# A two-layer hybrid trunk on one core: weight slots of the token-wise blocks shifted by 448 bytes, three raw buffers for four, and transposes moved out of the 256-column matmul streams

## Chip, cores, metric

One core of one Trainium2 chip. The time is the device time of one execution in microseconds, and it is compared as the median of several executions. Inputs and weights lie in the chip's memory as float32, and the output goes back there.

## What is computed

Two layers; in each, the 256 tokens of 1024 channels pass a gated feed-forward block, a mixer and another feed-forward block, each followed by a LayerNorm of `alpha*x + block(x)`. Cut to what matters:

```python
def swiglu(x, w1, w2):
    g, u = jnp.split(x @ w1, 2, axis=-1)          # w1: 1024 x 5632, w2: 2816 x 1024
    return (jax.nn.silu(g) * u) @ w2

def hybrid_mixer(x, w_in, b_merge, sc_w, rc_w, rc_b, rg_w, rg_b, a_param, w_out_conv, w_out_rnn, w_o):
    b_gate, c_gate, v, x_r, y_r, g_logits = jnp.split(x @ w_in, SPLITS, axis=-1)
    y_a = (b_gate * causal_depthwise_conv(c_gate * v, sc_w, 3)) @ w_out_conv
    xc = causal_depthwise_conv(x_r, rc_w, 4) + rc_b
    gates = jax.nn.sigmoid(per_head(xc, rg_w) + rg_b)         # 4 heads of 256
    h = rg_lru(xc, gates[0], gates[1], a_param)               # a scan over the tokens
    y_b = (h * jax.nn.gelu(y_r)) @ w_out_rnn
    g_a, g_b = jnp.split(jax.nn.sigmoid(g_logits + b_merge), 2, axis=-1)
    return (g_a * y_a + g_b * y_b) @ w_o

for l in range(2):
    x = layer_norm(ALPHA * x + 0.5 * swiglu(x, ffn_w1[l, 0], ffn_w2[l, 0]), ...)
    x = layer_norm(ALPHA * x + hybrid_mixer(x, ...), ...)
    x = layer_norm(ALPHA * x + 0.5 * swiglu(x, ffn_w1[l, 1], ffn_w2[l, 1]), ...)
```

## The kernel before

**Precision by three products.** Every float32 matrix is split into two parts in a matmul format (`F32R`): `hi`, the rounded value, and `lo`, what rounding left. A product is the sum hi·hi + hi·lo + lo·hi, so each matmul of the mathematics is three on TensorE.

**Units of weights.** All weights stream through the core once, in units of 1 MB (128 partitions x 2048 floats). `load_unit` takes a buffer `raw` (pool `praw`, `NRAW` of them) and one each of `hi` and `lo` (six of each, `NBUF`), and issues the load on SyncE's queue. `high` makes `hi` on ScalarE (L202), `low` makes `lo` on VectorE (L207); when `low` is done the raw buffer is free for a later load. Units are issued in the program's order, up to six (`LOOK`) ahead of those that TensorE has used up.

**Two forms of matmul.** In the channel-wise form (`mm_cols`, L219) a 128x128 piece of the weights is the stationary operand and 256 tokens of x (or of an intermediate) are the moving one: 256 columns, output transposed, channels on partitions. One unit is 48 such matmuls. In the token-wise form, 128 tokens are stationary and 512 columns of the weights move. The second matmul of each block (`form_b`, tile `acc`) has this form, and so have the first weight units of every block (`filler`, tile `fill`): token-wise they can begin on the first half of the tokens while the LayerNorm of the second half still runs.

**What follows the fill.** Its output has tokens on partitions and has to be transposed by TensorE (fp32 matmuls against an identity) for what comes next. In a feed-forward block `fill_transposes` (tile `hT`, L439) does this for the h of the first 256 channels, one step into the `gu` stream (gate and up projections); the first feed-forward block has two such fill blocks (`NFILL`), the others one. In the mixer the fill is 512 columns of the x_r projection; `x_transposes` (L500) turns them back in two groups of four, one behind `c0` and one behind `v0` of the order `MIX`.

**The order.** `MIX` lists the mixer's steps: `c v b` and `wc` are the gated convolution and its output projection, `x` and `rg` the recurrent branch, `sqrt` and `lru` its elementwise part and scan (VectorE, with some ScalarE), `y` the gelu branch, `ga gb` the merging gates, `wr` the recurrent output projection. `form_b` closes each block: its first units run over all outputs, the last three (`LAG`) output by output, so that LayerNorm can begin early. The steps are handed to a scheduler, which may move independent instructions past each other on an engine, matmuls too.

**Intermediates** lie in slots of 2 KB per partition (pool `act`, `NSLOT` of them), or, for eight of the wide ones, in the constant tiles `yh` and `yl`, from where `wc`, `rg` and `wr` take them as moving operand and `form_b` as stationary one (with a shift of 16 floats, L457).

**Addresses.** In the built program of before, taken modulo 512 bytes, xh, xl, yh and yl rows begin at 128, and all hi and lo buffers at 192; yh and yl rows with the shift of 16 floats, and all slots, at 192. So in `acc` the moving and the stationary operand begin at the same place modulo 512 (192 and 192); in `fill` they do not (weights 192, x 128), nor in the 256-column streams (x 128, weights 192).

**The start.** `opening` warms TensorE up and takes the first two units in halves; the loads go on one queue in this order: x and units 0 and 1, six small loads of bias and gate vectors (`load_vectors`), then units 2, 3, and so on.

Of the kernel before, what the change touches and what calls it, by code (L numbers as in the profile page):

```python
# [13 lines left out]

P = 128
NBUF = 6
NRAW = 4
NSLOT = 14
LAG = 3
LOOK = 6  # L20
WARM = 8
# [2 lines left out]
MIX = [  # L24
    (t.rstrip("0123"), int(t[-1]) if t[-1].isdigit() else 0)
    for t in (
        "c0 x0 v0 x1 x2 x3 rg0 c1 rg1 b0 v1 rg2 b1 rg3 sqrt c2 v2 b2 c3 v3 b3 lru0 gb0 lru1 "
        "wc0 wc1 wc2 lru2 wc3 ga0 ga1 lru3 ga2 ga3 y0 y1 y2 y3 gb1 gb2 gb3 wr0 wr1 wr2 wr3"
    ).split()
]  # L30

# [1 line left out]
class Unit:  # L33


    def __init__(self, srcs, shape):
        self.srcs, self.shape = srcs, shape


@with_exitstack  # L40
def trunk_kernel(
# [137 lines left out]
    def unit_half(parts, h):  # L179

        n = 512 // len(parts)
        srcs = []
        for i, (w, c0) in enumerate(parts):
            s = w[h * 512 : (h + 1) * 512, c0 : c0 + n].rearrange("(k p) c -> p k c", p=P)
            srcs.append((i * n, s))
        return unit(srcs, (4, 512))

    def load_unit(u, parts=1):
        u.raw = praw.tile([P, 2048], F32, tag="raw", name="raw")
        u.hi = phi.tile([P, 2048], F32R, tag="hi", name="hi")  # L190
        u.lo = plo.tile([P, 2048], F32R, tag="lo", name="lo")
        view = lambda t: t.rearrange("p (a b) -> p a b", b=u.shape[-1])
        u.h, u.l = view(u.hi), view(u.lo)
        n = u.shape[0] // parts
        for i in range(parts):
            ks = slice(i * n, (i + 1) * n)
            for c0, src in u.srcs:
                u.load = nc.sync.dma_start(out=view(u.raw)[:, ks, c0 : c0 + src.shape[-1]], in_=src[:, ks])
# [9 lines left out]
        gate[1] = max(gate[1] - 1, 0)  # L208

    def emit_unit(u):  # L210
        load_unit(u)
        high(u)
        low(u)

# [84 lines left out]
            elif t == 0:  # L299
                transpose_x(t, hh)  # L300

    def form_b(us, stat, c, l, n, last):

        Q = len(us)
        cuts = [[(0, 512), (512, 512)] for _ in range(NT)]
        if last:
            cuts[NT - 1] = [(0, 512), (512, 256), (768, 256)]
        acc = {}

        def pe(q, t, i):  # L310
            c0, n_ = cuts[t][i]
            if q == 0:
                acc[t, i] = bank("acc")[:, :n_]
            for kk in range(2):
                sh, sl = stat(q, kk, t)
                wh, wl = us[q].h[:, kk, c0 : c0 + n_], us[q].l[:, kk, c0 : c0 + n_]
                mm(acc[t, i], sh, wh, q == 0 and kk == 0, False)
                mm(acc[t, i], sl, wh, False, False)
                mm(acc[t, i], sh, wl, False, q == Q - 1 and kk == 1)

        for q in range(Q - LAG):
            step(lambda q=q: [pe(q, t, i) for t in range(NT) for i in range(len(cuts[t]))],
                 (lambda: load_gb(l, n, us[0])) if q == 0 else None, 1, [us[q]])
        for t in range(NT):
            for i in range(len(cuts[t])):
                for q in range(Q - LAG, Q):
# [77 lines left out]
    def ffn(l, i, n, last):  # L404
        w1, w2 = ffn_w1[l, i], ffn_w2[l, i]
        hs = {}
        opens = (l, i) == (0, 0)
        nfill = NFILL if opens else 1
        fill = [unit_half([(w1, 256 * b), (w1, DFF + 256 * b)], h) for b in range(nfill) for h in range(2)]
        ga, up = {}, {}  # L410
        for j in range(nfill, NPF):
            ga[j] = unit_a(w1, 256 * j)
            up[j] = unit_a(w1, DFF + 256 * j)
        us = [unit_b(w2, q) for q in range(NPF)]

        def swish(g, u, shape, name):

            v = slot(name)
            o = v.rearrange("p a b -> p (a b)")[:, : shape]
            nc.scalar.activation(o, g, AF.Tanh, scale=0.5)  # L420
            nc.vector.scalar_tensor_tensor(o, o, 1.0, g, op0=ALU.add, op1=ALU.mult)
            nc.vector.tensor_mul(o, o, u)  # L422
            return v

        tok = {}

        def post_fill(t, b, ps):
            tok[t, b] = swish(ps[:, 0:256], ps[:, 256:512], 256, "hf")

        filler(fill, post_fill, not opens)  # L430

        def fill_transposes(b):
            ps = bank("hT")
            h, lo = slot("h0h", F32R), slot("h0l", F32R)
            for t in range(NT):
                v = tok[t, b].rearrange("p a b -> p (a b)")
                for c in range(2):
                    with tc.issue_after(last_mm[0]):
                        nc.tensor.transpose(  # L439
                            ps[:, c * S + t * P : c * S + (t + 1) * P], v[:, c * P : (c + 1) * P], ident  # L440
                        )
# [23 lines left out]
        form_b(us, lambda q, kk, t: [v[:, kk, t * P : (t + 1) * P] for v in hs[q]], 0.25, l, n, last)  # L465


    def mixer(l, n):
        w = w_in[l]
        fill = [unit_half([(w, 3 * D)], h) for h in range(2)]  # L470
        cols = {"c": (w, D), "v": (w, 2 * D), "b": (w, 0), "x": (w, 3 * D), "y": (w, 4 * D), "ga": (w, 5 * D), "gb": (w, 6 * D),
                "wc": (w_out_conv[l], 0), "wr": (w_out_rnn[l], 0)}
        U = {}
        for key, j in MIX:
            if key in cols and (key, j) not in (("x", 0), ("x", 1)):
# [10 lines left out]
        B = {}  # L486

        def post_fill(t, b, ps):
            T["xt", t, b] = slot("xt").rearrange("p a b -> p (a b)")
            nc.scalar.copy(T["xt", t, b], ps)  # L490

        filler(fill, post_fill, True)

        def x_transposes(j):
            B["x", j] = bank("x")
            for c in range(2):
                for t in range(NT):
                    o = (j % 2) * 256 + c * P
                    with tc.issue_after(last_mm[0]):
                        nc.tensor.transpose(  # L500
                            B["x", j][:, c * S + t * P : c * S + (t + 1) * P], T["xt", t, j // 2][:, o : o + P], ident
                        )

        def proj(key, j):
# [79 lines left out]
        def lru(hd):  # L584


            s, y, e = T["s", hd], T["y", hd], T["xc", hd]
            d, q, a = slot("d"), slot("q"), slot("a")
            nc.scalar.activation(q, y, AF.Square)
            nc.vector.scalar_tensor_tensor(d, s, 1.0, y, op0=ALU.add, op1=ALU.mult)  # L590
            nc.vector.reciprocal(d, d)
            nc.vector.tensor_add(q, q, s)
            nc.vector.tensor_mul(q, q, d)
            nc.scalar.activation(a, q, AF.Square)
            nc.vector.scalar_tensor_tensor(a, s, 1.0, a, op0=ALU.add, op1=ALU.mult)
            nc.scalar.activation(a, a, AF.Copy, scale=-0.5, bias=1.0)
            nc.vector.tensor_mul(q, q, e)
            nc.vector.tensor_copy(q[:, :, 0:1], e[:, :, 0:1])
            for c in range(2):
                nc.vector.tensor_tensor_scan(d[:, c, :], a[:, c, :], q[:, c, :], 0.0, op0=ALU.mult, op1=ALU.add)  # L600
            T["h", hd] = d

        def post_y(j):

# [48 lines left out]
        for key, j in MIX:  # L653
# [2 lines left out]
                step(None, sqrt_all)  # L656
            elif key == "lru":
                step(None, lambda j=j: lru(j))
            elif key == "x" and j < 2:
                step(lambda j=j: x_transposes(j), after)  # L660
# [68 lines left out]
```

## Time and profile before

| | us |
|---|---|
| median of 3 executions | 1221.95 |
| the three | 1215.23, 1221.95, 1225.82 |
| the profiled execution: its time | 1216.33 |
| its span, first to last instruction | 1214.6 |
| TensorE matmul busy / weight loads busy | 1203.7 / 1138.0 |
| VectorE / ScalarE / GpSimd busy | 820.1 / 590.8 / 14.9 |
| granted TensorE clock, mean | 0.998 |
| DMA | 236.31 MB, mean 195 GB/s |

TensorE is busy 99% of the span, yet a busy engine is not one at its best pace: matmuls overlap, so how long one lasts says less than how far apart the starts are. A row of the timeline or of the chain of waits that merges N matmuls of a kind gives this: its length divided by N. Times in the chain are where the pieces of the chain that ended last begin and how long they are.

### The profile page before, as it was taken

How to read it: one execution, taken by the hardware profiler on the slowest of the kernel's cores; microseconds unless marked ns; L12 is line 12 of the kernel's file. 1: busy time of each engine (PE TensorE's matmuls, PEld its weight loads, DVE VectorE, ACT ScalarE, POOL GpSimd, SP SyncE). 2: the span in 40 equal slices, each digit the busy share in tenths (PEclk: the TensorE clock that was granted, in tenths of full speed). 3: DMA queues.
4: the chain of work that ended last, by engine and by line, in shares of the span. 5: the costliest groups of instructions: out<-in, count | busy, mean ns of one | idle time of the engine just before them, and what ended most of it. 6: DMA issues, size and time to landing. Idle time of an engine off the chain costs nothing.

```text
span 1214.6 us, 20489 instructions
## 1 busy us (share of the span) xinstructions
PE 1203.7 (99%) x8995; PEld 1138.0 (94%) x8995; DVE 820.1 (68%) x786; ACT 590.8 (49%) x566; POOL 14.9 (1%) x20
## 2 busy tenths in 40 slices
PE   8999999999999999999999999999999999999997
PEld 6999988999999899998899998899999998999986
DVE  5865547957997785564585554578789966856533
ACT  5644334775575354443254443266756744544420
POOL 0000000000000000000000000000000000000000
PEclk9999999999999999999999999999999999999999
DMA  8966563756566566655566655555665753856510
GB/s 282 328 217 217 176 205 100 248 186 229 176 209 213 169 194 218 215 207 177 169 194 217 216 207 177 170 187 174 223 206 184 243 175 103 278 188 229 201 43 35
DMA packets 186133, 236.31 MB, mean 195 GB/s; under 512 B 4076, under 2 KB 168124, under 8 KB 186044
## 3 DMA queue, kind: packets, MB, share of 16 engines
q1 hardware_dynamic: 186044, 235.00, 58.7%
q8 instruction: 70, 1.15, 0.4%
q14 instruction: 19, 0.16, 0.0%
HBM read 233.94 MB, written 1.05 MB: 193 GB/s over the span
## 4 chain that ended last, share of the span: by engine, by line
PE 97%; DMA 1%; DVE 0%; ACT 0%; SPq 0%; issue 0%; DVEq 0%; ACTq 0%
PE gu L216 35%; PE acc L216 23%; PE fill L216 5%; PE c L216 4%; PE v L216 4%; PE wr L216 4%; PE gb L216 4%; PE y L216 4%; PE ga L216 4%; PE wc L216 4%; PE b L216 4%; PE x L216 2%; PE rg L216 2%; DMA raw<-in_ffn_w_dram 1%; PE xT L262 1%; DVE lo L207 0%
## 5 line engine op out<-in xcount | busy, mean ns | idle before, releaser
L207 DVE TENSOR_TENSOR lo<-raw,hi 128x2048 fp32r<-128x2048 f32 (+1 forms) x218 | 493.5, 2269 | 231.9 <-ACT hi L202 230.7
L202 ACT CAST hi<-raw 128x2048 fp32r<-128x2048 f32 (+1 forms) x217 | 411.4, 1901 | 453.0 <-issue 170.0
L216 PE MATMUL gu<-xh,hi 128*128 128x256 f32 x1248 | 168.6, 277 | 0.0
L216 PE MATMUL gu<-xh,lo 128*128 128x256 f32 x1248 | 168.0, 277 | 0.0
L216 PE MATMUL gu<-xl,hi 128*128 128x256 f32 x1248 | 168.0, 277 | 0.0
L216 PEld LDWEIGHTS gu<-xh,hi 128*128 128x128 f32 x1248 | 154.5, 188 | 0.3
L216 PEld LDWEIGHTS gu<-xl,hi 128*128 128x128 f32 x1248 | 154.1, 188 | 0.0
L216 PEld LDWEIGHTS gu<-xh,lo 128*128 128x128 f32 x1248 | 154.1, 188 | 0.0
L216 PE MATMUL acc<-hi,hl 128*128 128x512 f32 (+1 forms) x196 | 73.8, 376 | 0.0
L216 PE MATMUL acc<-hi,hh 128*128 128x512 f32 (+1 forms) x196 | 73.7, 376 | 0.0
L216 PE MATMUL acc<-lo,hh 128*128 128x512 f32 (+1 forms) x196 | 73.7, 376 | 0.0
L422 DVE TENSOR_TENSOR hv<-hv,gu 128x512 f32<-128x512 f32 x39 | 26.8, 688 | 53.4 <-PE gu L216 53.2
L216 PE MATMUL acc<-hi,yh 128*128 128x512 f32 (+1 forms) x136 | 51.5, 379 | 0.0
L216 PE MATMUL acc<-hi,yl 128*128 128x512 f32 (+1 forms) x136 | 51.3, 377 | 0.0
L216 PE MATMUL acc<-lo,yh 128*128 128x512 f32 (+1 forms) x136 | 51.3, 377 | 0.0
L266 ACT CAST xh<-xT 128x512 fp32r<-128x512 f32 x24 | 13.4, 588 | 75.2 <-PE xT L262 74.8
L288 DVE SCALAR_TENSOR_TENSOR xtok<-acc,xtok 128x512 f32<-128x512 f32 (+1 forms) x25 | 16.7, 668 | 46.6 <-PE acc L216 46.3
L216 PEld LDWEIGHTS acc<-lo,hh 128*128 128x128 f32 x196 | 36.9, 188 | 6.8
L216 PEld LDWEIGHTS acc<-hi,hh 128*128 128x128 f32 x196 | 36.9, 188 | 6.7
L216 PEld LDWEIGHTS acc<-hi,hl 128*128 128x128 f32 x196 | 36.9, 188 | 6.7
L216 PE MATMUL fill<-hi,xh 128*128 128x512 f32 x112 | 30.6, 395 | 2.1 <-ACT hi L202 1.1
L216 PE MATMUL fill<-lo,xh 128*128 128x512 f32 x112 | 30.8, 397 | 0.2 <-DVE lo L207 0.2
(181 smaller groups left out, 1826.6 us busy)
## 6 DMA issues: line engine op xcount, KB each, us to landing
raw<-in_ffn_w_dram SPq DMA_DIRECT2D x122, 1024.0 KB, 5.2
raw<-in_w_in_dram SPq DMA_DIRECT2D x56, 1024.0 KB, 5.2
raw<-in_ffn_w_dram SPq DMA_DIRECT2D x16, 512.0 KB, 4.9
raw<-in_w_out_conv_dram SPq DMA_DIRECT2D x8, 1024.0 KB, 5.5
raw<-in_w_out_rnn_dram SPq DMA_DIRECT2D x8, 1024.0 KB, 5.5
raw<-in_w_o_dram SPq DMA_DIRECT2D x8, 1024.0 KB, 5.0
raw<-in_rg_w_dram SPq DMA_DIRECT2D x4, 1024.0 KB, 5.4
gB<-in_ln_g_dram SPq DMA_DIRECT2D x6, 512.0 KB, 6.3
```

Of the source, the lines that this page charges most:

```text
L202: (copy or nc.scalar.copy)(u.hi[:, part], u.raw[:, part])
L207: nc.vector.tensor_sub(u.lo[:, part], u.raw[:, part], f(u.hi[:, part]))
L216: last_mm[0] = nc.tensor.matmul(ps, lhs, rhs, start=first, stop=last).ins
L262: nc.tensor.transpose(ps[:, i * P : (i + 1) * P], xtok[:, t, c * P : (c + 1) * P], ident)
L266: nc.scalar.copy(dh, v)
L288: nc.vector.scalar_tensor_tensor(zc, ps, c, zc, op0=ALU.mult, op1=ALU.add)
L422: nc.vector.tensor_mul(o, o, u)
```

## The change

1. `NRAW` 4 to 3, `NSLOT` 14 to 15. Each hi and lo buffer grows by `PAD` = 128 floats, and units made by `unit_half` (those of the fills) begin `OFF` = 112 floats = 448 bytes into theirs. In the built program hi and lo buffers still begin at 192 modulo 512; the fill's weights then begin at 128, like the rows of x that they are multiplied with. No other operand moves modulo 512.
2. `fill_transposes` goes from the `gu` stream into `form_b`, behind its second unit; `form_b` takes the units in the order qs, so that the fill's h come eighth (first block: seventh and eighth).
3. In the mixer the fill is the first 512 columns of the g_b gate instead of x_r. `x0` and `x1` become ordinary units; `gb0` and `gb1` are transposed just before `wr0`, in one group of eight. `gb0` no longer stands behind `lru0`, and `sqrt` stands later.
4. `lru` works in place: its outputs overwrite s, its temporaries y and d. The operations are the same in number and size; Square now follows the first VectorE operation in place of going beside it.
5. Unit 2 is loaded ahead of the small vectors.

```diff
-NRAW = 4
-NSLOT = 14
+NRAW = 3
+NSLOT = 15
+PAD = 128
+OFF = 112
...
-        "c0 x0 v0 x1 x2 x3 rg0 c1 rg1 b0 v1 rg2 b1 rg3 sqrt c2 v2 b2 c3 v3 b3 lru0 gb0 lru1 "
-        "wc0 wc1 wc2 lru2 wc3 ga0 ga1 lru3 ga2 ga3 y0 y1 y2 y3 gb1 gb2 gb3 wr0 wr1 wr2 wr3"
+        "c0 x0 x1 v0 x2 x3 rg0 c1 rg1 b0 v1 rg2 b1 rg3 c2 v2 b2 c3 v3 b3 sqrt lru0 lru1 "
+        "wc0 wc1 wc2 lru2 wc3 ga0 ga1 lru3 ga2 ga3 y0 y1 y2 y3 gb2 gb3 gb0 gb1 wr0 wr1 wr2 wr3"
...
-        return unit(srcs, (4, 512))
+        u = unit(srcs, (4, 512))
+        u.off = OFF
+        return u
...
-        u.hi = phi.tile([P, 2048], F32R, tag="hi", name="hi")
-        u.lo = plo.tile([P, 2048], F32R, tag="lo", name="lo")
+        u.hi = phi.tile([P, 2048 + PAD], F32R, tag="hi", name="hi")[:, u.off : u.off + 2048]
+        u.lo = plo.tile([P, 2048 + PAD], F32R, tag="lo", name="lo")[:, u.off : u.off + 2048]
...
         for q in range(Q - LAG):
             step(lambda q=q: [pe(q, t, i) for t in range(NT) for i in range(len(cuts[t]))],
                  (lambda: load_gb(l, n, us[0])) if q == 0 else None, 1, [us[q]])
+            if q == 1 and between:
+                step(between)
...
-        us = [unit_b(w2, q) for q in range(NPF)]
+        qs = list(range(nfill, NPF - LAG)) + list(range(nfill)) + list(range(NPF - LAG, NPF))
+        us = [unit_b(w2, q) for q in qs]
...
             step(lambda j=j: pe(j, 0, ga[j]), None, 1, [ga[j]])
-            if 1 <= j - nfill <= nfill:
-                step(lambda b=j - nfill - 1: fill_transposes(b))
             step(lambda j=j: pe(j, 1, up[j]), lambda j=j: post(j), 1, [up[j]])
...
+        def first_blocks():
+            for b in range(nfill):
+                fill_transposes(b)
...
-        fill = [unit_half([(w, 3 * D)], h) for h in range(2)]
+        fill = [unit_half([(w, 6 * D)], h) for h in range(2)]
...
-        def x_transposes(j):
-            B["x", j] = bank("x")
+        def gb_transposes(j):
+            B["gb", j] = bank("gb")
...
-            s, y, e = T["s", hd], T["y", hd], T["xc", hd]
-            d, q, a = slot("d"), slot("q"), slot("a")
-            nc.scalar.activation(q, y, AF.Square)
-            nc.vector.scalar_tensor_tensor(d, s, 1.0, y, op0=ALU.add, op1=ALU.mult)
+            s, q, e = T["s", hd], T["y", hd], T["xc", hd]
+            d = slot("d")
+            nc.vector.scalar_tensor_tensor(d, s, 1.0, q, op0=ALU.add, op1=ALU.mult)
+            nc.scalar.activation(q, q, AF.Square)
...
     for hh in range(2):
         load_x(hh)
         load_unit(units[hh], 2)
+    load_unit(units[2])
     with tc.issue_after(units[1].load.ins):
         load_vectors()
```

What the diff does not show is where the scheduler puts things. Three places matter.

**TensorE, first feed-forward block.** Before, the four transposes of a fill block (`hT`) stand between two `gu` units:

```order
L216 MATMUL gu<-xh,hi 128x256 x8
L216 MATMUL gu<-xl,hi 128x256 x8
L216 MATMUL gu<-xh,lo 128x256 x8
L439 MATMUL hT<-ident,hf 128x128 x4
L216 MATMUL gu<-xh,hi 128x256 x8
L216 MATMUL gu<-xl,hi 128x256 x8
```

and now both groups stand between the 512-column matmuls of the second and third unit of `form_b`:

```order
L221 MATMUL acc<-hi,hh 128x512
L221 MATMUL acc<-hi,hl 128x512
L221 MATMUL acc<-lo,hh 128x512
L447 MATMUL hT<-ident,hf 128x128 x8
L221 MATMUL acc<-hi,hh 128x512
L221 MATMUL acc<-hi,hl 128x512
```

No transpose is left in the `gu` streams; the other three feed-forward blocks have one group of four, at the same place.

**TensorE, first mixer, behind the last unit of `b`.** Here yh and yl hold the convolution's output, which the work behind `b3` on VectorE and ScalarE completes, `hi_…` and `lo_…` are weights, and `wc_…` are the banks of `wc0`, `wc1` and so on. Before, `gb0` stands between:

```order
L216 MATMUL b_2884<-xh_78,lo_2574 128x256 x8
L216 MATMUL gb_2957<-xh_78,hi_2638 128x256 x8
L216 MATMUL gb_2957<-xl_79,hi_2638 128x256 x8
L216 MATMUL gb_2957<-xh_78,lo_2639 128x256 x8
L216 MATMUL gb_2957<-xh_78,hi_2638 128x256 x8
L216 MATMUL gb_2957<-xl_79,hi_2638 128x256 x8
L216 MATMUL gb_2957<-xh_78,lo_2639 128x256 x8
L216 MATMUL wc_3030<-yh_80,hi_2701 128x256 x8
L216 MATMUL wc_3030<-yl_81,hi_2701 128x256 x8
```

Now `wc0` follows at once, and the scheduler mixes the parts of `wc0`, `wc1` and `wc2` that need only the first six blocks of yh and yl:

```order
L221 MATMUL b_2976<-xh_78,lo_2674 128x256 x8
L221 MATMUL wc_3068<-yh_80,hi_2730 128x256 x6
L221 MATMUL wc_3125<-yh_80,hi_2793 128x256 x6
L221 MATMUL wc_3182<-yh_80,hi_2851 128x256 x3
L221 MATMUL wc_3068<-yh_80,hi_2730 128x256 x2
L221 MATMUL wc_3068<-yl_81,hi_2730 128x256 x6
L221 MATMUL wc_3125<-yh_80,hi_2793 128x256 x2
L221 MATMUL wc_3125<-yl_81,hi_2793 128x256 x6
L221 MATMUL wc_3182<-yh_80,hi_2851 128x256 x4
L221 MATMUL wc_3068<-yl_81,hi_2730 128x256 x2
```

Fifteen matmuls stand ahead of the first that needs `b3`'s yh, and 35 ahead of the first that needs its yl.

On ScalarE the square roots, which ran four units earlier before, now come just ahead of that yh:

```order
L549 ACTIVATE cvc<-cs,vec 128x256 x2
L592 ACT_TABLE_LOAD
L592 ACTIVATE y<-s,tiny 128x512 x3
L206 CAST hi<-raw 128x2048
L243 CAST yh<-cvc 128x512
```

A table load and three of the four square roots have moved in ahead of the `hi` that stands before `b3`'s yh.

**SyncE, the start of the program.** `rows` are the small vectors. Before, units 2 and 3 (four loads of halves) stand behind all six of them:

```order
L198 DMA raw<-in_ffn_w_dram 128x2x256 x4
L129 DMA rows<-in_b_merge_dram 16x2x128
L129 DMA rows<-in_sc_w_dram 24x2x128
L129 DMA rows<-in_rc_w_dram 32x2x128
L129 DMA rows<-in_rc_b_dram 8x2x128
L129 DMA rows<-in_rg_b_dram 16x2x128
L129 DMA rows<-in_a_param_dram 8x2x128
L198 DMA raw<-in_ffn_w_dram 128x4x256 x4
```

Now the two loads of unit 2 stand ahead of them:

```order
L202 DMA raw<-in_ffn_w_dram 128x2x256 x4
L202 DMA raw<-in_ffn_w_dram 128x4x256 x2
L131 DMA rows<-in_b_merge_dram 16x2x128
L131 DMA rows<-in_sc_w_dram 24x2x128
L131 DMA rows<-in_rc_w_dram 32x2x128
L131 DMA rows<-in_rc_b_dram 8x2x128
L131 DMA rows<-in_rg_b_dram 16x2x128
L131 DMA rows<-in_a_param_dram 8x2x128
L202 DMA raw<-in_ffn_w_dram 128x4x256 x2
```

Only unit 3 is still behind the vectors.

More of the change, by code (lines that the diff above doesn't have):

```diff
@@ L36, in __init__ @@
     def __init__(self, srcs, shape):
-        self.srcs, self.shape = srcs, shape
+        self.srcs, self.shape, self.off, self.raw = srcs, shape, 0, None
 @with_exitstack
@@ L210, in emit_unit @@
     def emit_unit(u):
-        load_unit(u)
+        if u.raw is None:
+            load_unit(u)
         high(u)
@@ L300, in layer_norm, with form_b @@
                 transpose_x(t, hh)
-    def form_b(us, stat, c, l, n, last):
+    def form_b(us, stat, c, l, n, last, between=None):
         Q = len(us)
@@ L460, in ffn @@
             step(lambda j=j: pe(j, 0, ga[j]), None, 1, [ga[j]])
-            if 1 <= j - nfill <= nfill:
-                step(lambda b=j - nfill - 1: fill_transposes(b))
             step(lambda j=j: pe(j, 1, up[j]), lambda j=j: post(j), 1, [up[j]])
-        form_b(us, lambda q, kk, t: [v[:, kk, t * P : (t + 1) * P] for v in hs[q]], 0.25, l, n, last)
+        def first_blocks():
+            for b in range(nfill):
+                fill_transposes(b)
+        form_b(us, lambda q, kk, t: [v[:, kk, t * P : (t + 1) * P] for v in hs[qs[q]]], 0.25, l, n, last, first_blocks)
     def mixer(l, n):
         w = w_in[l]
-        fill = [unit_half([(w, 3 * D)], h) for h in range(2)]
+        fill = [unit_half([(w, 6 * D)], h) for h in range(2)]
         cols = {"c": (w, D), "v": (w, 2 * D), "b": (w, 0), "x": (w, 3 * D), "y": (w, 4 * D), "ga": (w, 5 * D), "gb": (w, 6 * D),
@@ L474, in mixer @@
         for key, j in MIX:
-            if key in cols and (key, j) not in (("x", 0), ("x", 1)):
+            if key in cols and (key, j) not in (("gb", 0), ("gb", 1)):
                 U[key, j] = unit_a(cols[key][0], cols[key][1] + 256 * j)
@@ L488, in post_fill @@
         def post_fill(t, b, ps):
-            T["xt", t, b] = slot("xt").rearrange("p a b -> p (a b)")
-            nc.scalar.copy(T["xt", t, b], ps)
+            T["gt", t] = slot("gt").rearrange("p a b -> p (a b)")
+            nc.scalar.copy(T["gt", t], ps)
         filler(fill, post_fill, True)
-        def x_transposes(j):
-            B["x", j] = bank("x")
+        def gb_transposes(j):
+            B["gb", j] = bank("gb")
             for c in range(2):
@@ L500, in x_transposes @@
                         nc.tensor.transpose(
-                            B["x", j][:, c * S + t * P : c * S + (t + 1) * P], T["xt", t, j // 2][:, o : o + P], ident
+                            B["gb", j][:, c * S + t * P : c * S + (t + 1) * P], T["gt", t][:, o : o + P], ident
                         )
@@ L593, in lru @@
             nc.vector.tensor_mul(q, q, d)
-            nc.scalar.activation(a, q, AF.Square)
-            nc.vector.scalar_tensor_tensor(a, s, 1.0, a, op0=ALU.add, op1=ALU.mult)
-            nc.scalar.activation(a, a, AF.Copy, scale=-0.5, bias=1.0)
+            nc.scalar.activation(d, q, AF.Square)
+            nc.vector.scalar_tensor_tensor(d, s, 1.0, d, op0=ALU.add, op1=ALU.mult)
+            nc.scalar.activation(d, d, AF.Copy, scale=-0.5, bias=1.0)
             nc.vector.tensor_mul(q, q, e)
@@ L599, in lru @@
             for c in range(2):
-                nc.vector.tensor_tensor_scan(d[:, c, :], a[:, c, :], q[:, c, :], 0.0, op0=ALU.mult, op1=ALU.add)
-            T["h", hd] = d
+                nc.vector.tensor_tensor_scan(s[:, c, :], d[:, c, :], q[:, c, :], 0.0, op0=ALU.mult, op1=ALU.add)
+            T["h", hd] = s
         def post_y(j):
@@ L658, in mixer @@
                 step(None, lambda j=j: lru(j))
-            elif key == "x" and j < 2:
-                step(lambda j=j: x_transposes(j), after)
+            elif key == "gb" and j < 2:
+                step(lambda j=j: gb_transposes(j), after)
             elif key == "rg":
```

## The prediction

> **What bounds the kernel now.** I read the chain of waits first. TensorE has nearly all of it, so a gain on another engine counts only where TensorE waits for it:
>
> ```profile
> span 1214.6 us, 20489 instructions
> PE 97%; DMA 1%; DVE 0%; ACT 0%; SPq 0%; issue 0%; DVEq 0%; ACTq 0%
> ```
>
> So the question is at what pace TensorE runs and where it stops. For the pace I read the pieces of the chain, one behind the other (start, length, what, how many):
>
> ```profile
> 33.34 16.34 PE gu L216 x144
> 61.46 73.49 PE gu L216 x624
> 201.57 6.42 PE fill L216 x28
> 208.00 5.66 PE c L216 x48
> 456.66 92.51 PE gu L216 x816
> 549.17 55.77 PE acc L216 x246
> 816.29 11.31 PE x L216 x96
> 827.60 2.98 PE rg L216 x24
> 1036.86 16.96 PE gu L216 x144
> ```
>
> The same matmul of 256 columns has two paces. In the piece at 456.66 it takes 92.51/816 = 113.4 ns, at 61.46 it takes 73.49/624 = 117.8 ns, through all 624. The slow pace sits in five pieces: against 113.3 ns each, 61.46 costs 2.8 us, 1036.86 costs 0.6, 816.29 and 827.60 together 0.7 (some of it a wait, below), 208.00 costs 0.2: **4.3 us** in this execution. A pace begins where a stream begins: behind the fill (fast at 33.34, slow at 208.00 and 1036.86) or behind a group of transposes (fast at 456.66, slow at 61.46). Once begun it lasts until something interrupts the stream. Around 827 us, the row at 827.79 starts 0.36 us behind the one before it, where two matmuls take 0.24, and the next pair 0.34 later; from 828.37 on the pairs come every 0.23:
>
> ```profile
> 827.43 0.40 PE L216 MATMUL rg<-yh,hi 128*128 128x256 f32 x2
> 827.79 0.51 PE L216 MATMUL rg<-yl,hi 128*128 128x256 f32 x2
> 828.13 0.40 PE L216 MATMUL rg<-yh,lo 128*128 128x256 f32 x2
> 828.37 0.39 PE L216 MATMUL rg<-yh,hi 128*128 128x256 f32 x2
> 828.60 0.39 PE L216 MATMUL rg<-yl,hi 128*128 128x256 f32 x2
> ```
>
> So a short wait turned a slow stream into a fast one. Fifteen streams begin in this program behind a fill or a transpose, and four of them are slow: each is a draw. If all 7200 matmuls of 256 columns were slow, that would be 7200 x 4.5 ns = 32.4 us; 4 draws of 15 are 8.6 us on average, and this execution had 4.3 because it drew well on the long streams. The spread of the three executions (1215.23 to 1225.82) is of that size, which fits, though one trace does not show it.
>
> The 512-column matmuls differ too: `fill` takes 6.42/28 = 229.3 ns, `acc` 55.77/246 = 226.7 ns. Both have 512 columns; what differs is that in `acc` both operands begin at the same place modulo 512 bytes, in `fill` not.
>
> **The fill, shifted by 448 bytes.** It now has the addresses that `acc` has, so I take `acc`'s pace: 336 matmuls x 2.6 ns = **-0.8 us** (bounds: 0, if the addresses are not the cause, and -0.9).
>
> What matters more is the pace in which the stream behind it begins. The nearest thing in the trace is the last block, where `acc` goes from 512 columns to 256:
>
> ```profile
> 1150.46 0.39 PE L216 MATMUL acc<-lo,h0h 128*128 128x512 f32 x1
> 1150.69 0.28 PE L216 MATMUL acc<-hi,h0h 128*128 128x256 f32 x1
> 1150.81 0.28 PE L216 MATMUL acc<-hi,h0l 128*128 128x256 f32 x1
> 1150.92 0.28 PE L216 MATMUL acc<-lo,h0h 128*128 128x256 f32 x1
> 1151.04 0.28 PE L216 MATMUL acc<-hi,h0h 128*128 128x256 f32 x1
> 1151.16 0.28 PE L216 MATMUL acc<-hi,h0l 128*128 128x256 f32 x1
> ```
>
> From 1150.69 to 1150.92 two take 0.23 us, so 115 on average, and from 1150.92 on 0.12 each. Here both operands stay at the same place modulo 512, and 120 ns is where it ends; in `gu` they do not (128 against 192), and there 113.4 is a pace that holds itself. I read it so: behind a stream of `acc`'s steadiness the first 256-column matmul is still fast, and `gu` stays as it starts. Then the streams behind the fill are all fast, and since points 2 and 3 leave no transposes in them, they stay fast to the end of `gu`, and in the mixer to `wc0`. That is **-4.3 us** against this execution, with the bounds in the rivals.
>
> What stays a draw: behind the new wait at `wc0` 672 matmuls (`wc`, `ga`, `y`, `gb2`, `gb3`), and behind the eight transposes 192 (`wr`), in each mixer. 2 x 864 x 4.5 ns x 4/15 = **+2.1 us**; bounds 0 and +7.8.
>
> The Trainium skill speaks against this (TensorE: Matmul & The Clock Gate, Step-by-step: what each phase is for): TensorE reads the moving operand and the weights through two independent ports, and loading the next weights takes no read bandwidth from the running matmul. By that rule addresses can't matter, the fill gains nothing, and the draws stay as they are; the rival for it is below. The trace does not bear it out plainly, since 624 equal matmuls took 117.8 ns and 816 others 113.4, but it doesn't name the cause.
>
> **Transposes moved.** Their number stays (5 groups of four for h, 16 for the mixers), and so does the cost of a group, which the chain shows:
>
> ```profile
> 61.03 0.44 PE hT L439 x4
> ```
>
> A group also delays the first matmul behind it by about 0.1 us, in 256 as in 512 columns. Two groups become one in each mixer and in the first block: **-0.3 us** (bounds 0, -0.5). `form_b` gives hT a place five units ahead of the one that uses it, some 27 us by 24 x 226.7 ns each, ample for one copy and one subtraction (0.6 and 0.7 us): nothing.
>
> **The start.** Unit 2 lands late because it stands behind the vectors, and meanwhile the DMA engines idle (second row: share 0.27):
>
> ```profile
> 9.00:12.00 3.00, 3.00 (x16) 2.46 (x15) 1.69 (x2) 0.34 (x1) 0.00 (x0) 1.00 1.03 349
> 12.00:14.50 2.50, 2.50 (x16) 1.99 (x14) 1.38 (x3) 2.14 (x4) 0.00 (x0) 1.00 0.27 71
> 19.38 1.90 ACT L202 CAST hi<-raw 128x2048 fp32r<-128x2048 f32 x1 [4.05 <-DMA raw<-in_ffn_w_dram]
> 19.13 1.08 PE L216 MATMUL fill<-lo,xh 128*128 128x512 f32 x4
> 21.33 1.20 PE L216 MATMUL fill<-hi,xh 128*128 128x512 f32 x4 [1.12 <-ACT hi L202]
> 23.66 1.21 PE L216 MATMUL fill<-lo,xh 128*128 128x512 f32 x4 [0.22 <-DVE lo L207]
> ```
>
> TensorE could go on at 19.13 + 4 x 0.23 = 20.05 and does at 21.33; at 23.66 it waits once more, 0.22 us, and each restart costs about 0.1. Issued ahead of the vectors, unit 2 follows unit 1 without a break; 1 MB at the 349 GB/s of the first row is 3.0 us, so it lands near 16 in place of 19.3. Its hi (1.9 us) and lo (2.3) are then done near 20.3, and lo is needed at 20.05 + 8 x 0.23 = 21.9. **-1.7 us** (bounds -1.0, if the vectors then hold up unit 3, and -1.9).
>
> Three raw buffers: unit 5 now waits for unit 2's lo, near 20 by this, and is needed only when the fill (48 matmuls behind 20.05, to 31) and unit 4 are done, past 36. Later a load waits for the lo three units earlier in place of four. That leaves three units, 3 x 5.44 = 16.3 us, for a lo (2.3), a load and a hi (1.9):
>
> ```profile
> raw<-in_w_in_dram SPq DMA_DIRECT2D x56, 1024.0 KB, 5.2
> ```
>
> 5.2 us to land leaves 6.9 to spare, and behind that five finished units. Nothing; if that cover were gone, every microsecond of a late load would be one of TensorE's.
>
> **`wc0` behind `b3`.** `gb0` hid what follows `b3` on the other engines. `b3` gives TensorE free at 296.01; then:
>
> ```profile
> 296.01 1.07 PE L216 MATMUL gb<-xh,hi 128*128 128x256 f32 x8
> 295.30 1.92 ACT L202 CAST hi<-raw 128x2048 fp32r<-128x2048 f32 x1 [2.72 <-PE b L216]
> 296.21 0.69 DVE L549 TENSOR_TENSOR cvc<-cvc,b 128x512 f32<-128x512 f32 x1 [0.53 <-PE b L216]
> 297.12 0.62 ACT L238 CAST yh<-cvc 128x512 fp32r<-128x512 f32 x1
> 297.25 2.29 DVE L207 TENSOR_TENSOR lo<-raw,hi 128x2048 fp32r<-128x2048 f32 x1 [0.35 <-ACT hi L202]
> 299.46 0.68 DVE L239 TENSOR_TENSOR yl<-cvc,yh 128x512 fp32r<-128x512 f32 x1
> ```
>
> yh is there 1.7 us after `b3`, yl 4.1 us (the `lo` of 2.29 us stands between on VectorE). In the new order 15 matmuls (1.7 us) stand ahead of the need for yh and 35 (4.0 us) ahead of that for yl: so some 0.2 us of waiting. But a table load and three square roots now stand ahead of that `hi` on ScalarE, in the 2.72 us that it idled:
>
> ```profile
> L582 ACT ACT_TABLE_LOAD x2 | 2.6, 1283 | 0.0
> L582 ACT ACTIVATE y<-s,tiny 128x512 f32<-128x512 f32 x8 | 5.1, 713 | 0.0
> ```
>
> 1.28 + 3 x 0.71 = 3.4 us, 0.7 more than it had; if all of that comes through, the wait is 0.9. I take 0.6 in each mixer, **+1.2 us** (bounds 0 and +2). `wr0` now has two units and the transposes, 12 us, between it and `y3`, whose yl came 10.7 us after it (it ends where `gb1` begins):
>
> ```profile
> 366.73 1.07 PE L216 MATMUL gb<-xh,hi 128*128 128x256 f32 x8
> 376.17 1.29 DVE L239 TENSOR_TENSOR yl<-gv,yh 128x512 fp32r<-128x512 f32 x2
> ```
>
> `wr0` needs them 2.3 us after it begins, which leaves 3.5; I count nothing and price the case below.
>
> **Sum**, against the profiled execution, 1216.33 us (span 1214.6 and 1.7 around it), which lies 5.6 under the median of the three: 1216.33 - 0.8 - 4.3 + 2.1 - 0.3 - 1.7 + 1.2 = **1212.5 us**. Its own range, 1208.5 to 1217, comes from the bounds of the draws that stay and of the waits.
>
> **Rivals.**
> - *The draws stay.* Behind the shifted fill a stream still begins fast or slow. For it: behind the fill 2 of 6 are slow, behind transposes 2 of 9, much the same, so the cause may lie in neither. Against it: `acc` never changes its pace. Then 8.6 us stand in place of 2.1 and this execution's 4.3: 1219.0. By the page's rule of two ports it is this, with 0.8 more for the fill.
> - *The other side: always slow.* If a steady 512-column stream always leaves `gu` in the slow pace, as its 256-column tail ends at 120 ns, then 864 + 3 x 960 + 2 x 864 = 5472 matmuls lose 4.5 ns, 24.6 us, with no transposes left to end it: 1212.5 + 24.6 = 1237, slower than before. It decides from about 2700 matmuls on (12 us over the sum is beyond the median of before). Against it: in that tail both operands begin at the same place, in `gu` they don't.
> - *VectorE late in the mixer.* Without `gb0`, `y3` comes 5.44 us earlier against VectorE's `lru` work, of which one `lo` (2.3) falls away: 3.1 us less slack, out of some 3.5 at `wr0`. If it is used up twice in each mixer, up to 1.5 us each: 1218.5.
>
> **How the numbers follow.** Fast streams 0.55, draws 0.27, always slow 0.08, VectorE late 0.10. The range of 8 in 10 takes the first, nearly all of the fourth and two thirds of the second: 1208 to 1224. 1% of 1221.95 is 12.2 us, about what a measurement of this kernel can tell from no change. Under 1209.7 lies a fifth of the first case and a little of the second: faster 0.15. Over 1234.2 lies the third: slower 0.08. Same 0.77.
>
> **What would show it.** Right: `fill` pieces of 28 near 6.35 us; every `gu` piece whole, 960 in 108.8 us (864 in 97.9); `c` to `b3` of the mixers at 113.3; the `fill` behind 20.05 us without a wait; two waits under 1 us at `wc0`. Wrong: a `gu` piece near 113 us for 960, which is the slow pace; a TensorE wait over 1 us at `wr0` or in `form_b` behind hT.

## The result, and the profile after

The changed kernel takes **1234.87 us** (median of four: 1234.21, 1234.85, 1234.89, 1238.47) against 1221.97 before (four: 1215.23 to 1225.82): ratio 1.0118 over all executions, 95% interval 1.0069 to 1.0166. It is slower, by about 1%, and outside the predicted range of 1208 to 1224. The profiled execution of after took 1234.21 us, 17.9 more than that of before.

TensorE still has nearly the whole chain, and the only waits that the profile gives its matmuls are the two of the opening (second fence; columns: us in total, times, longest):

```profile
span 1232.4 us, 20480 instructions
...
PE 99%; DVE 0%; issue 0%; DVEq 0%; ACT 0%
```

```profile
PE warm L260 <- DVE mhalf L691: 1.4, 1, 1.4
PE fill L221 <- DVE hi L206: 1.0, 1, 1.0
```

So no new wait explains 18 us; the pace must. The chain of waits, the same pieces as shown of before (start, length, what, how many):

```profile
30.77 101.76 PE gu L221 x864
...
199.99 6.36 PE fill L221 x28
206.35 5.66 PE c L221 x48
212.00 11.31 PE x L221 x96
...
330.40 21.76 PE ga L221 x192
...
442.27 113.07 PE gu L221 x960
...
1051.12 113.07 PE gu L221 x960
```

Every `gu` stream is whole now, and every one is slow from its first matmul to its last: 113.07/960 = 117.8 ns, and 101.76/864 the same. The mixers are slow from `c0` (11.31/96) up to `wc0`, and fast behind it (`ga`: 21.76/192 = 113.3). That is the rival "always slow". Its price was 5472 x 4.5 ns = 24.6 us. Summed over the starts in the trace, the slow matmuls of after (115.5 to 141 ns from one start to the next) lose 24.66 us against 113.3 ns each, those of before 4.28.

The other terms can be read beside it. The fill is steady now (6.36/28 = 227 ns, 6.42/28 before). Unit 2 lands at 16.1 in place of 19.3, the DMA engines don't pause behind unit 1 (last columns: granted clock, DMA share, GB/s), and the fill goes on without a wait:

```profile
9.00:12.00 3.00, 3.00 (x19) 2.56 (x18) 1.31 (x2) 0.65 (x2) 0.00 (x0) 1.00 1.08 366
12.00:14.50 2.50, 2.50 (x14) 1.90 (x13) 1.89 (x3) 2.50 (x4) 0.00 (x0) 1.00 1.08 342
```

```profile
16.13 1.91 ACT L206 CAST hi<-raw 128x2048 fp32r<-128x2048 f32 x1 [1.32 <-DMA raw<-in_ffn_w_dram]
...
19.50 1.07 PE L221 MATMUL fill<-hi,xh 128*128 128x512 f32 x4
```

At `wc0` there is the short wait that was forecast, on the side of the weight loads (PEld): yh comes 0.23 us late, and the stream behind it is fast (`ga` above):

```profile
307.95 2.46 PE L221 MATMUL wc<-yh,hi 128*128 128x256 f32 x17
309.23 0.62 ACT L243 CAST yh<-cvc 128x512 fp32r<-128x512 f32 x1
309.90 0.30 PEld L221 LDWEIGHTS wc<-yh,hi 128*128 128x128 f32 x2 [0.23 <-ACT yh L243]
```

A step below is the time from one matmul's start to the next one's, taken from the starts of the single records in the trace. The last three steps of each fill, the last one up to the first matmul of the stream behind it, in ns:

| stream begins (before) | steps | pace | begins (after) | steps | pace |
|---|---|---|---|---|---|
| 33.17 | 231 226 236 | 113.3 | 30.61 | 227 227 225 | 117.8 |
| 207.83 | 230 231 227 | 117.8 | 206.19 | 227 226 226 | 117.8 |
| 439.71 | 226 229 231 | 113.3 | 442.11 | 226 227 226 | 117.8 |
| 622.01 | 226 229 231 | 113.3 | 628.59 | 227 227 226 | 117.8 |
| 804.31 | 226 229 231 | 113.3 | 815.05 | 226 227 226 | 117.8 |
| 1036.70 | 229 232 226 | 117.8 | 1050.95 | 227 227 226 | 117.8 |

Before, the fill goes round through 226, 229 and 231, and the two streams that began behind a last step of 226 or 227 are the slow ones. After, the fill stands still at 226.7, and each last step is of that kind (225 to 227). I call the place in its round at which the fill stands when the stream takes over the phase of the hand-over; the last step is the sign by which it is read. This was in the trace of before, and the prediction had not looked at it.

### The profile page after: what moved, and what is told of

Its sections match the earlier page's. It is cut to its first block, busy times and chain, and to the rows that moved or that the text cites. A ratio compares the mean times of both kernels' runs of the same rounds, so it can differ in the third digit from the quotient of the medians.

```text
span 1232.4 us, 20480 instructions
## 1 busy us (share of the span) xinstructions
PE 1222.9 (99%) x8995; PEld 1158.1 (94%) x8995; DVE 821.4 (67%) x786; ACT 590.6 (48%) x566; POOL 14.9 (1%) x20
## 4 chain that ended last, share of the span: by engine, by line
PE 99%; DVE 0%; issue 0%; DVEq 0%; ACT 0%
PE gu L221 36%; PE acc L221 23%; PE fill L221 6%; PE b L221 4%; PE c L221 4%; PE x L221 4%; PE v L221 4%; PE wc L221 4%; PE wr L221 4%; PE y L221 4%; PE ga L221 4%; PE rg L221 2%; PE gb L221 2%; PE xT L267 1%; PE warm L260 0%; PE hT L447 0%
## 5 line engine op out<-in xcount | busy, mean ns | idle before, releaser
L221 PE MATMUL gu<-xh,lo 128*128 128x256 f32 x1248 | 172.5, 281 | 0.0
L221 PE MATMUL gu<-xh,hi 128*128 128x256 f32 x1248 | 172.4, 281 | 0.0
L221 PE MATMUL gu<-xl,hi 128*128 128x256 f32 x1248 | 172.4, 281 | 0.0
L221 PEld LDWEIGHTS gu<-xh,hi 128*128 128x128 f32 x1248 | 158.7, 189 | 0.3
L221 PEld LDWEIGHTS gu<-xh,lo 128*128 128x128 f32 x1248 | 158.1, 189 | 0.0
L221 PEld LDWEIGHTS gu<-xl,hi 128*128 128x128 f32 x1248 | 157.9, 189 | 0.0
```

The lines of the kernel that those rows point to most:

```text
L221: last_mm[0] = nc.tensor.matmul(ps, lhs, rhs, start=first, stop=last).ins
```

## The experiments

Three theories stood at first: the shifted ("aligned") fill, whose two operands begin at the same place, hands over the slow pace (H); the new layout of the buffers is slow (L); or the alignment has nothing to do with it and only the interruptions are missing (U). All edits but the third are made to the changed kernel. The kernel before ran in each set on the same chip; its own median was 1221.3, 1214.4, 1215.1 and 1221.2 us in the four timed sets, so times are compared within a set.

### The shift undone: e1_off0

```diff
-OFF = 112
+OFF = 0
```

> The changed kernel with one number undone: the fill's weights start again 192 bytes off modulo 512 (x at 128), everything else as changed. Theory H (hand-over): a fill with both operands at the same place modulo 512 leaves every 256-column stream behind it in the slow pace, and a fill that isn't aligned leaves it a draw, 2 of 6 slow as before the change. Then fill pieces of 28 go back to 6.42 us or more, some of the six streams run at 113.3 ns, and with a third of the 24.7 us left the time is about 1219 us (1211 to 1228). Rival L (layout): the new spacing of the weight buffers and the third raw buffer make the streams slow. Then all six stay at 117.8 ns and the time stays near 1235. Rival U (uninterrupted): the fill's alignment is nothing to it, each stream is a draw, and the changed kernel only lacks the interruptions that would draw anew; then also about 1219, and e3 must part it from H.

1219.25 us (1211.86 to 1222.76), ratio to before 0.9978 (0.9941 to 1.0015). All six streams of the profiled execution are fast, and the fill is back at 6.42 or 6.43 for 28:

```profile
31.70 97.94 PE gu L221 x864
...
197.09 6.43 PE fill L221 x28
...
436.85 108.83 PE gu L221 x960
```

Layout, three raw buffers and every other point were as in the changed kernel, so L falls. The other points together are worth nothing that can be told from zero; with the shift on top of them they are a loss.

### Four transposes between fill and stream: e2_kick

```diff
+    def kick():
+        ps = bank("kick")
+        for i in range(4):
+            with tc.issue_after(last_mm[0]):
+                nc.tensor.transpose(ps[:, i * P : (i + 1) * P], ident, ident)
...
+        step(kick)
```

`step(kick)` stands ahead of the loop of the `gu` steps and ahead of that over `MIX`.

> The changed kernel with four transposes of the identity into a spare bank between each aligned fill and the 256-column stream behind it (six places), which nobody reads. H and U: the stream now begins behind transposes, where 7 of 9 were fast before the change; the interruption costs 6 x 0.55 = 3.3 us. All six fast: 1234.2 - 24.7 + 3.3 = 1213; with 2 of 9 slow 1218. L: the streams stay slow and the time is 1237 or 1238.

1218.4 us (1215.48 to 1221.22), ratio 0.9971 (0.9936 to 1.0007). The fill stays aligned, and all six streams are fast:

```profile
435.89 1.37 PE fill L221 x6
437.26 0.44 PE kick L257 x4
437.69 2.41 PE gu L221 x21
```

```profile
437.69 108.83 PE gu L221 x960
```

So the slow pace isn't in the aligned fill's data or buffers but in how the stream behind it is entered. The ten times lie at 1215.5 (two), 1218.1 to 1218.5 (five) and 1221.1 to 1221.2 (three): steps of 2.9 us, which fits the draw that is left behind `wc0` in each mixer (672 x 4.5 ns = 3.0). Only one execution of the lowest group was profiled, so that is argued and not shown.

### The first point alone, on the kernel before: e3_part1_on_before

```diff
-NRAW = 4
-NSLOT = 14
+NRAW = 3
+NSLOT = 15
+PAD = 128
+OFF = 112
...
+        u.off = OFF
```

`unit_half` and `load_unit` are as in the change, all else as before.

> The kernel before with the first point of the change alone: three raw slots, the longer weight buffers, the fill's weights shifted by 448 bytes; all transposes where they were. H: all six 256-column streams begin at 117.8 ns and keep it up to their first interruption (gu 144 matmuls in 17.0 us in place of 16.3, then the transposes draw anew); fill pieces of 28 near 6.45 or less. The time is then that of before, within its draws: 1222 (1217 to 1230). U: the first pieces are a draw, two or so of six slow. L: slow before and behind the transposes alike, 7200 x 4.5 ns = 32 us, of which before had 4.3: near 1244.

1225.3 us (1224.54 to 1225.99), ratio 1.0021 (0.9989 to 1.0052). All six streams begin slow, and the transposes end it only here and there:

```profile
31.80 16.96 PE gu L220 x144
49.20 11.31 PE gu L220 x96
60.95 70.74 PE gu L220 x624
...
436.55 16.96 PE gu L220 x144
453.95 96.11 PE gu L220 x816
```

16.96/144 = 117.8; behind the first transposes still 11.31/96 = 117.8, behind the second 70.74/624 = 113.4. U falls: six of six, where before had two. It took both halves of the change to lose 24.7 us: the shift makes every stream begin slow, and the transposes that were moved out had ended that in part (slow matmuls lose 14.7 us in this execution). That they end it wasn't to be counted on: four of the five `hT` entries here stay slow, where before four of five were fast.

### Another shift: e4_off64 and e8_off64_timed

```diff
-OFF = 112
+OFF = 64
```

> The changed kernel with the fill's weights shifted by 256 bytes in place of 448: they start at 448 modulo 512 and x at 128, neither aligned nor as before. H as I have it (only equality counts): the fill runs at about 229.3 ns per matmul, the streams behind are draws as with no shift, about 1219. If every shift away from 192 makes the fill steady at 226.7 ns and the streams slow, then equality isn't the condition: near 1235. L: near 1235 whatever the fill does. U: a draw.

> The changed kernel with the fill's weights shifted by 256 bytes in place of 448 (as looked at once, 1211.4), timed. H: behind an unaligned fill the six streams are all fast, and only the streams behind the waits at wc0 and behind gb's transposes are draws: 1211.4 with both fast, up to 2 x 864 x 4.5 ns = 7.8 us more: median 1212 to 1219, below before by 0.3 to 0.9%. U: the six streams are draws too: spread as before, 1212 to 1230.

One execution took 1211.37 us, with everything fast, and I took it for the version to have. Timed on another chip the same kernel took 1220.65 (1217.7 to 1231.43), ratio 1.0061 (1.0038 to 1.0083): slower than before, whose median there was 1214.4. In this profile two of the six streams are slow, the first and the last:

```profile
31.21 101.76 PE gu L221 x864
...
440.13 108.83 PE gu L221 x960
...
1038.01 113.07 PE gu L221 x960
```

Their fills ended in steps of 230 231 **227** and 229 232 **226**; the other four in 226 229 231 or 225 230 230. In e4's profile, of the same code with the same addresses, the first and the last fill ended in 232 225 236 and 226 229 231, and the streams behind them were fast. My expectation that an unaligned fill makes all six fast failed; it leaves each to the step in which it happens to end.

### Only one half of each fill aligned: e6_half_aligned

```diff
-        fill = [unit_half([(w1, 256 * b), (w1, DFF + 256 * b)], h) for b in range(nfill) for h in range(2)]
+        fill = [unit_half([(w1, 256 * b), (w1, DFF + 256 * b)], h, OFF * h) for b in range(nfill) for h in range(2)]
...
-        fill = [unit_half([(w, 6 * D)], h) for h in range(2)]
+        fill = [unit_half([(w, 6 * D)], h, OFF * (1 - h)) for h in range(2)]
```

> The changed kernel with one half of each fill's weights shifted: in the ffns only the second half (the 12 matmuls that end at the 256-column stream are aligned, the 12 before them are not), in the mixers only the first half (the last 12 are not aligned). H, if what stands just ahead of the stream hands over the pace: the four gu streams are slow (117.8: 960 in 113.1 us, 864 in 101.8), the two mixer streams (c to b3) are free again, as with no shift, likely 113.3. That is 24.7 - 2 x 864 x 4.5 ns = 16.9 us over the fast case, near 1227 to 1230. If the whole fill counts or its first half: the mixers slow, the ffns not, near 1219. U: draws without order.

1228.46 us (one execution), as H had it: twelve aligned matmuls just ahead of the stream (24 in the first block) are enough for the slow pace, twelve unaligned ones behind aligned ones give the fast one, in both mixers with the same steps (232 226 236):

```profile
31.57 101.76 PE gu L221 x864
...
207.26 5.46 PE c L221 x48
212.72 10.88 PE x L221 x96
...
439.74 113.07 PE gu L221 x960
```

### The streams' own addresses: e5_scan and e7_scan_fine

```diff
+AOFF = [16, 32, 48, 64, 80, 112]
...
+        u.off = AOFF[stage[0]]
```

`stage[0]` counts the six blocks from 0, and the line stands in `unit_a` and at the `rg` units. The finer scan has `AOFF = [8, 24, 20, 28, 4, 12]`.

> The changed kernel with the weights of the 256-column streams moved too, by another amount in each of the six stages, so that they start 128, 192, 256, 320, 384 and 0 bytes beyond x modulo 512 (64 in the changed kernel); the fill stays aligned, and form_b as it was. If a pace belongs to the relation of the two operands: the last stage (0, both at the same place) runs its gu at 120 ns, as the 256-column tail of acc does: 960 in 115.2 us; and among the five others some have one pace only, 113.3 ns (960 in 108.8 us) or another, whatever the fill hands over. If the hand-over alone decides: all five are at 117.8 (113.1 us for 960, 864 in 101.8). H says nothing between these; I expect 117.8 in the five and 120 in the last, 1237 in all. L: as H.

1250.91 us (one execution). Half of what I expected failed: not only the stage with equal addresses runs at 120.0 ns.

```profile
31.38 103.69 PE gu L225 x864
...
214.54 11.31 PE x L225 x96
...
448.48 115.19 PE gu L225 x960
...
637.11 113.07 PE gu L225 x960
...
829.33 11.52 PE x L225 x96
...
950.22 22.78 PE ga L225 x192
...
1065.65 115.19 PE gu L225 x960
```

Weights beyond x by 128, 256, 384 or 0 bytes: 103.69/864 = 120.0, 115.19/960 = 120.0, 11.52/96 = 120.0, all behind the fill. By 192 or 320: 117.8, as with 64. So the relation counts modulo 128 bytes. Where it is 64, there are two paces, 113.3 and 117.8. Where it is zero there are two as well: behind the wait at `wc0` the second mixer (384 bytes) goes on at 22.78/192 = 118.6, and stays there to the end of `wr`. None of these pieces is at 113.3.

> As the scan by 64 bytes before, but with finer steps: in the six stages the weights of the 256-column streams start 96, 160, 144, 176, 80 and 112 bytes beyond x modulo 512, that is 96, 32, 16, 48, 80 and 112 modulo 128; the fill stays aligned. The scan showed one pace, 120.0 ns, wherever the two operands differ by a multiple of 128 bytes, and 117.8 behind an aligned fill where they differ by 64 more. If the relation modulo 128 decides with a step of 64: all six stages run at 117.8 behind the aligned fill (864 in 101.8, 960 in 113.1 us) and near 1235 in all. If the relation grades it: each stage has a pace of its own between 113.3 and 120, and one may be fast without a kick. If there is one at 113.3 here, a version with the aligned fill and without draws is to be had, near 1210.

1251.61 us (one execution). The stages of 96, 16 and 48 bytes:

```profile
31.46 101.38 PE gu L225 x864
...
449.90 115.19 PE gu L225 x960
...
638.50 113.36 PE gu L225 x960
```

The relation grades it: 16, 32 and 112 bytes give 120.0 (115.19/960 for 16), 48 gives 118.1, 80 gives 118.7 and 96 gives 117.3, all behind the aligned fill; none gives 113.3.

The prediction weighed the rule of the Trainium skill (TensorE: Matmul & The Clock Gate, Step-by-step: what each phase is for) that the weights' port takes nothing from the moving operand's, and read it so that addresses can't matter. Read so, these two runs, in which TensorE's instructions are those of the changed kernel in the same order and only addresses differ, should cost what that kernel costs; they cost 16 and 17 us more. The measurement decides against applying the rule to this pace; it doesn't show what the two operands share.

### A phase that can be set: e10_half_back, e11_half_back_gb2

By now the theory was P: behind a fill, the phase in which it ends decides; its rival D is a plain draw behind any unaligned fill. In e10 the second half of every fill loses its shift; e11 has gb2 between `b3` and `wc0` as well.

```diff
-        u.off = OFF
+        u.off = OFF * (1 - h)
```

> The changed kernel with the shift of the second half of each fill undone (the half that ends at the 256-column stream starts 192 bytes off again, the first half stays aligned). Theory P (phase): an unaligned 512-column stream goes round through three steps (226, 229, 231 ns), and the 256-column stream behind it is slow when the last step is 226 or 227 and fast when it is 231; an aligned stream stands still at 226.7 and so hands over the slow case always. Then 12 or 24 unaligned matmuls behind an aligned, standing stream always end in the same step: as the mixers of the half-aligned run did (232 226 236, then fast), all six are fast in every execution. Draws are left only behind wc0 (672 matmuls, 3.0 us) and behind gb's transposes (192, 0.9 us) in each mixer: 1211.5 with both fast, at most 7.8 more, and the executions lie within 8 us. D (a plain draw behind any unaligned fill): executions spread over 20 us, median 1215 to 1222. Before, on the same chip, draws between 1211 and 1230.

> As the run with the second half's shift undone, and gb2 ahead of wc0 (one block of 48 matmuls between b3 and wc0, as gb0 was before the change). The waits at wc0 (0.5 us in each mixer) go, and with them the draw behind them: the stream stays as it came, fast. P: 1 us under e10 at its best, 1210.5, and what is left is the draw behind gb's transposes (0.9 us in each mixer): all executions within 2 us, 1210.5 to 1212.5. If slots are short because gb2's gate is held longer, TensorE waits somewhere in the mixer, 1 us or more, and a new draw begins there.

e10: 1219.24 us (1214.99 to 1222.40), ratio 1.0021 (0.9998 to 1.0045). Five of the six streams are fast, each behind 231 or 232, 225 or 226, 235 or 236, and the executions lie within 7.4 us. But the opening stream is slow, in the profiles of e10 and e11 alike (here e10):

```profile
31.30 101.76 PE gu L221 x864
...
439.38 108.82 PE gu L221 x960
```

There the fill ends with 24 unaligned matmuls in place of 12, and its last steps are 229 232 **226** (227 in e11). P holds, and my count of "12 or 24" as one case was wrong. e11: 1217.05 (1213.10 to 1218.06), ratio 1.0008 (0.9989 to 1.0028). The waits at `wc0` are gone, but gb2 is missing between `y3` and `wr0`, and yh comes late there:

```profile
381.12 0.68 DVE L622 TENSOR_TENSOR gv<-gv,s 128x512 f32<-128x512 f32 x1
381.77 1.89 ACT L206 CAST hi<-raw 128x2048 fp32r<-128x2048 f32 x1
383.56 1.13 ACT L243 CAST yh<-gv 128x512 fp32r<-128x512 f32 x2
384.23 0.50 PE L221 MATMUL wr<-yh,hi 128*128 128x256 f32 x2 [1.08 <-ACT yh L243]
```

The step on that side of `wr0` is 1.36 us long, 1.25 too many, in each mixer. That is the loss of slack that the prediction priced as the rival "VectorE late" (up to 1.5 us each), and the changed kernel itself escaped it. The engine is another, though: VectorE had the gv of the first of these two yh done at 381.80 (first line), but ScalarE had begun a weight unit's `hi` at 381.77, and both yh come behind it, from 383.56 on.

### The phases set, beside the changed kernel: e12_set_phases, e13_changed_again

```diff
-        "wc0 wc1 wc2 lru2 wc3 ga0 ga1 lru3 ga2 ga3 y0 y1 y2 y3 gb2 gb3 gb0 gb1 wr0 wr1 wr2 wr3"
+        "gb2 wc0 wc1 wc2 lru2 wc3 ga0 ga1 lru3 ga2 y0 y1 y2 y3 ga3 gb3 gb0 gb1 wr0 wr1 wr2 wr3"
...
-        u.off = OFF
+        u.off = OFF * (whole or 1 - h)
...
+        if opens:
+            step(kick)
```

`whole` and `opens` are true for the first block, and `kick` is that of e2.

> The version that theory P points to: the first fill wholly aligned with four transposes of the identity behind it (fast in the run with six of them), the other five fills with only their first half shifted (fast in 5 of 5), gb2 between b3 and wc0 (no wait there, so no draw), and ga3 behind y3, so that y3 to wr0 keep the distance that they have in the changed kernel (with gb2 alone moved, wr0 waited 1.36 us). P: every 256-column stream up to gb1 is fast in every execution; left is the draw behind gb's transposes (192 matmuls, 0.9 us in each mixer). From e10's 1215.0 at its best: 1215.0 - 3.9 (the opening gu) + 0.55 (the four transposes) - 1.1 (two waits at wc0) = 1210.6, and 1212.4 with both wr slow; all executions within 3 us, under before and the changed kernel alike. D: the spread stays at 8 us or more.

> The changed kernel as it is, on the chip of the run above. P: the aligned fill sets all six streams slow in every execution and on any chip, 5472 matmuls x 4.5 ns; only the 672 matmuls behind wc0 and the 192 behind gb's transposes of each mixer are draws. So 1234.2 with these fast, up to 1242 with all slow, and nothing below 1233, while before goes up and down between 1211 and 1230. D: now and then a stream is fast, some executions below 1230.

e12: **1210.19 us**, ratio 0.9928 (0.9897 to 0.9959), and its twelve executions lie between 1209.94 and 1210.66. Beside it the changed kernel took 1234.91 (1234.51 to 1238.73), ratio 1.0144 (1.0096 to 1.0191), and before 1221.16 (1210.92 to 1229.61). In e12 no 256-column piece is slow:

```profile
31.66 97.95 PE gu L221 x864
...
301.48 5.44 PE gb L221 x48
306.92 21.76 PE wc L221 x192
...
378.51 21.78 PE wr L221 x192
...
435.19 108.82 PE gu L221 x960
```

This version beats both kernels. It keeps the change but for the shift of five half fills and the place of two gate blocks, and adds four transposes. The spread is gone in these twelve executions. Behind the fills that was forecast by P. That `wr`, behind gb's transposes, is fast too (21.78/192 = 113.4) was not: its entry was left to chance, and no run gave a rule for it.

Over eleven profiles (without e2, where no stream follows a fill, and the two scans) 65 streams with weights 64 bytes from x modulo 128 begin behind a fill. The 28 whose fill ended in a step of 225 to 227 ns are all slow, the 37 with 230 to 236 all fast. Behind the aligned fill all of them are slow; behind the unaligned one both kinds occur, in one kernel and with equal addresses, so it is the phase and not the address of the fill that decides.

## Why the prediction was wrong

- **The fill's pace, -0.8:** right in kind. Its uninterrupted steps lost 0.79 us against 226.7 ns each before and lose 0.24 now: -0.6.
- **The step that failed, -4.3:** "behind a stream of `acc`'s steadiness the first 256-column matmul is still fast, and `gu` stays as it starts". It rested on the tail of the last block, where a first step near 113 ns was followed by 120. The scan shows that tail to be another case: with operands equal modulo 128 bytes `gu`, too, began with 113 or 114 ns behind the steady fill in two of its stages and went on at 120.0. With `gu`'s own addresses the first step behind the steady fill is 118 or 119 ns, and the pace is 117.8. Nor is the first step a sign of the pace: the streams that come out fast begin with 116 to 118 ns as well, and reach 113 only at about the sixth step. What holds of the second half of the sentence is that the pace, once reached, stays to the end of `gu`, here at the prediction's cost. The term is +20.4 (24.66 - 4.28) in place of -4.3 + 2.1.
- **Draws:** "behind the fill 2 of 6 are slow, behind transposes 2 of 9" was read as chance. Behind the fill it is the phase, and the six rows that tell it were in the trace of before. Behind transposes and behind the waits at `wc0` no run gave a rule that forecasts it; in the profiles of before, e3 and e13 both outcomes occur in one execution.
- **The draws that stay, +2.1:** in the profiled execution of after they all came out fast, by luck as far as is known, so only 0.3 of it stood (71 slow matmuls outside the six streams). In e13's profile the second mixer's came out slow, 28.3 us lost in place of 24.7, and that execution took 1238.54.
- **The rival "always slow", 0.08, 1237 us:** right in mechanism and size (24.6 forecast, 24.66 in all measured); 1237 holds the 2.1 us just named. The chance was too low because the argument against it was one tail with other addresses.
- **The smaller terms:** start -1.7, measured -1.9 (restarts and waits of the fill: 2.72 us lost before, 0.78 now). `wc0` +1.2, measured 0.7 (steps of about 300, 224 and 171 ns in place of 113.3 in each mixer). Transposes -0.3: the restarts in the 256-column streams, apart from `wc0`, lose 0.9 less (0.2 of it the short wait at `rg`), `acc` 0.4 more, the transposes themselves take 0.2 more: -0.3. These and the fill make -2.1; the warm-up and the transposes of x took 0.5 less as well, as they vary between executions (5.17 to 5.80 us for the eleven matmuls of the warm-up), and 20.4 - 2.6 = 17.8 is the difference of the two profiles (17.9).
- **Nothing for three raw buffers, `wr0` and hT in `form_b`:** right; the view of the waits has none of them.
- **The sum's own range, 1208.5 to 1217:** the bounds stated for the draws and the waits (0 to 7.8, 0 to 2) give 1209.2 to 1219.0. That changes nothing, since both lie under what was measured.

## What to carry to other kernels

Where matmuls of one shape show two paces in a trace, look at the steps just ahead of each stream before calling it chance: the phase at the hand-over may decide, and here it could be set by addresses or by four transposes in between. An edit that makes a stream steadier can make what follows it always bad, and taking interruptions out of a stream takes out what would have ended that. A single execution of a kernel with such draws says little (1211 and then 1220.65 for the same code); read the paces in the profile, and time it in several executions beside the kernel before.

## What the runs showed of the hardware

- A 128x128 by 256-column matmul of this format has at least three steady paces at nearly full granted clock (0.998 or 0.999 in every profile): 113.3, 117.8 and 120.0 ns. With the two operands equal modulo 128 bytes 120.0 was seen behind the fill and 118.6 behind one of the waits at `wc0` (e5); with 64 bytes between them, 113.3 or 117.8, kept over up to 960 matmuls.
- For 512 columns it is the other way round: in the fill, equal starts give the best pace, 226.7 ns and steady; with 64 bytes between them the steps go round through about 226, 229 and 231.
- Four transposes behind an aligned fill always led to the fast pace (seven of seven entries), behind slow or fast 256-column streams now to this, now to that. What in the hardware holds such a phase is open: no run here shows it.
